# Norm boundaries at high priority, early decay scalars, masks behind q's reciprocal norm and late norm-row broadcasts in a two-block f32 kernel

## The chip, the cores and the metric

The kernel runs on one core of a Trainium2 chip. The metric is the device time of one execution in microseconds (us): the median of several executions, 932.28 us before the change (three runs, 931.84 to 934.05).

## What is computed

Input x is 256 rows of 1024 floats (f32), and two different blocks follow one another. Weights and activations are f32.

```
first block:
  h    = rms_norm(x, pre_mix_norm);  proj = h @ w_in            # q, k, v | gdn q, k, v | z | a, b
  mix  = concat(softmax_attention(q, k, v, rel_bias),           # causal, 8 heads of 64
                gated_deltanet(conv(gdn qkv), z, a, b)) @ w_out  # chunks of 64
  x    = x + rms_norm(mix, post_mix_norm)
  h    = rms_norm(x, pre_mlp_norm)
  x    = x + rms_norm(square(relu(h @ w_up)) @ w_down, post_mlp_norm)
second block:
  h    = rms_norm(x, g_mix);  proj = h @ w_in_2
  x    = x + (gate_a * conv(...) @ w_a_out + gate_r * retention(q, k, v, dec_f, dec_b) @ w_r_out) @ w_o
  h    = rms_norm(x, g_ffn)
  x    = x + (silu(h @ w_ff_gate) * (h @ w_ff_up)) @ w_ff_down
  return rms_norm(x, g_final)
```

In gated_deltanet each chunk of 64 rows needs the solution of a unit lower triangular system, (I + m) uw = rhs, where m comes from the normalized k; q is divided by its norm as well. In the retention every head has a decay, log_sigmoid(dec_f) and log_sigmoid(dec_b), of which the kernel forms log(1 + exp(-|.|)).

## The kernel before, in words

**Matrix products.** Every large product is taken in three matmuls with fp32r operands: high part by high part, high by low, low by high. `load_w` (L207 to L218) fetches a 512 KB weight tile `raw` by a DMA from SP's queue (three buffers), ACT copies its high part into `wh` (the copy is recorded at L144), and DVE subtracts it, `wl` = raw - wh (L218). PE works on wh and wl at L222, or L294 for one kind of product. The activations stand transposed in `xT`, again as a high part, which ACT writes (L413), and a low part, which DVE writes (L416). PE fills PSUM banks of three names: `mm`, `sd` and `at`.

**What sets the order.** A tile scheduler orders each engine's instructions by priority, which is program order unless the code says otherwise, and by what is ready. `after(name)` (L167 to L176) puts the next instructions of an engine behind the instruction last recorded under that name: an edge in the order, not a wait by itself. SP issues the weight DMAs; POOL issues the small loads and the broadcasts, and does some elementwise work and all powers (reciprocal square roots).

**The head (up to about 30 us).** The first normalized rows are transposed, the first weight tiles come in, and POOL issues small loads: `rows` (conv weights), `hs` (A_log, dt_bias), three 256 KB tiles of constants `cs`, `relT`, and the four broadcasts `wb` of 256 KB: `row_bcast` (L178 to L185) reads a norm row of 1024 floats into two tiles of 128 x 512, the same on all partitions. `chan` holds the conv weights transposed; `lpl` is the logarithm that the gates g need, `R` is made of g and cs.

**The deltanet part (45 to 100 us).** POOL makes `kbe` and `kd` (L873 to L878), k scaled in two ways. `inv_norm` (L782) sums squares (`ssq`) and calls `rstd` (L400 to L403): DVE writes `ms`, POOL raises it to the power -1/2, `rnq` for q. DVE then scales q (`fq`, `fqd`, `qn`, `qd`), PE transposes the result (L795). The product m = `md` goes through memory into blocks of 16: `mb`. Four masked copies `b` of m (128 x 512 each, L893 to L896) are made on POOL for the levels 16 and 32. The solve inside the blocks (L932 to L937) is a chain of 15 steps of two DVE operations, `tmpb` and `tb`; its result goes through memory to `U` and `T`, which PE multiplies with the masks b. The convolution's `acc` steps run on DVE beside this.

**The boundaries.** Behind w_out (L1066 to L1074), w_down (L1118 to L1123) and w_o (L1278 to L1286) the product of each row tile t = 0, 1 is normalized and added to x (`post_norm_add`, L452 to L460, with squares `junk`, the power `r` on POOL L428, `pw` and the new x; behind w_o a plain addition), then `rms_T` normalizes x into the rows `xs` (L439, L441) and `row_T` (L447 to L452) transposes them on PE (L451) and splits them into xT. T0 and T1 below are these transposes for t = 0 and t = 1. The next product begins behind T0.

**The decay scalars.** `head_scalars` (L485 to L492) loads dec_f_2 and dec_b_2, a few values on each partition, and `log1p_exp_neg_abs` (L497 to L508) takes `lpa` = |.|, `lpu` = exp, and `lpl`, a logarithm for which ACT loads another function table. Both stand in the program behind the up stage.

## Time and profile before

| | before |
|---|---|
| median of 3 runs | 932.28 us (931.84 to 934.05) |
| profiled execution, its time | 932.19 us |
| its span | 930.4 us |
| instructions | 13880 |
| mean granted clock of PE | 0.994 |
| PE busy | 902.0 us (97%) |
| weight loads of PE (PEld) | 770.2 us (83%) |
| DVE busy | 600.1 us (64%) |
| ACT busy | 475.2 us (51%) |
| POOL busy | 81.2 us (9%) |

The span runs from the first to the last instruction of the profiled execution; the execution's own time is 1.8 us longer. Busy shares say how long an engine worked, not whether something waited for it: PEld overlaps PE, and what an engine waits for stands in a view of its own. PEclk is the clock that was granted to PE as a share of 2.4 GHz; 0.50 is 1.2 GHz. In the rows of a timeline stand start, duration, engine, line, operation, output and inputs, shapes and the number of instructions that were put together; in square brackets the idle time of the engine ahead of it and what ended that. All times are us from the start of the span, unless marked otherwise.

### The profile page before, as it was taken

To read this page: it belongs to the slowest core of one execution; us is meant where nothing else is said; L and a number is where in the kernel's file an instruction comes from. 1 tells how busy PE (TensorE), PEld (TensorE's weight loads), DVE (VectorE), ACT (ScalarE), POOL (GpSimd) and SP (SyncE) were. 2 spreads that over 40 slices of the span, in tenths; PEclk is the share of its full clock that TensorE was granted. 3 is DMA by queue.
4 is the path that set the end of the run, shared out by engine and by line. 5 is a ranking of instruction groups with operands and counts; after the bars stand their busy time and mean duration, and the time that the engine had idled before them with its cause. 6 is when DMAs were issued, how large, how long until landed. Compare 5 with 4: busy or idle time off the path is not lost.

```text
span 930.4 us, 13880 instructions
## 1 busy us (share of the span) xinstructions
PE 902.0 (97%) x5397; PEld 770.2 (83%) x5397; DVE 600.1 (64%) x885; ACT 475.2 (51%) x722; POOL 81.2 (9%) x96
## 2 busy tenths in 40 slices
PE   5999999989999999999999999999999999999997
PEld 4788887778888888799988888888888788888886
DVE  3888555376887563868666687844557657666543
ACT  4774373356766453645445555444344546555432
POOL 4072001030000000203200000000000000000000
PEclk9999999999999999999999999999999999999999
DMA  9673663147676665577646457666474567666551
GB/s 274 183 184 67 161 211 91 46 144 209 193 203 203 222 196 182 155 220 214 182 119 176 132 165 201 181 203 190 165 229 141 159 203 205 189 191 184 183 179 46
DMA packets 177138, 162.41 MB, mean 175 GB/s; under 512 B 18940, under 2 KB 144168, under 8 KB 177072
## 3 DMA queue, kind: packets, MB, share of 16 engines
q1 hardware_dynamic: 175200, 156.49, 57.3%
q0 software_dynamic: 1728, 4.78, 1.6%
q8 instruction: 42, 0.69, 0.3%
q10 hardware_dynamic: 144, 0.26, 0.1%
q14 instruction: 24, 0.20, 0.1%
HBM read 158.59 MB, written 2.92 MB: 174 GB/s over the span
## 4 chain that ended last, share of the span: by engine, by line
PE 85%; DMA 4%; POOL 3%; ACT 3%; DVE 3%; issue 2%; SPq 0%; POOLq 0%; ACTq 0%
PE mm L222 57%; PE at L222 18%; PE sd L222 6%; PE mm L294 2%; DMA raw<-in_w_in_dram 1%; POOL b L147 1%; ACT junk L424 1%; DVE wl L218 1%; PE sd L795 1%; POOL r L428 1%; DMA rows<-in_w_conv_dram 1%; DMA raw<-in_w_up_dram 1%; ACT wh L144 1%; DMA wb<-in_pre_mlp_norm_dram 1%; DMA x<-in_x_dram 0%
## 5 line engine op out<-in xcount | busy, mean ns | idle before, releaser
L218 DVE TENSOR_TENSOR wl<-raw,wh 128x1024 fp32r<-128x1024 f32 (+1 forms) x287 | 352.3, 1232 | 220.7 <-ACT wh L144 218.8
L144 ACT ACTIVATE wh<-raw 128x1024 fp32r<-128x1024 f32 (+1 forms) x287 | 301.8, 1056 | 293.5 <-PE at L222 69.5
L222 PE MATMUL mm<-xT,wh 128*128 128x256 f32 (+1 forms) x976 | 251.5, 334 | 1.4 <-ACT wh L144 1.4
L222 PEld LDWEIGHTS mm<-xT,wh 128*128 128x128 f32 x976 | 167.2, 193 | 21.0 <-ACT wh L144 1.6
L222 PE MATMUL mm<-wh,xT 128*128 128x512 f32 x528 | 168.6, 393 | 2.6 <-DVE xT L416 1.5
L222 PEld LDWEIGHTS mm<-wh,xT 128*128 128x128 f32 x528 | 98.7, 188 | 25.3 <-DVE xT L416 2.8
L222 PE MATMUL mm<-xT,wl 128*128 128x256 f32 x400 | 111.9, 280 | 0.0
L222 PE MATMUL mm<-wl,xT 128*128 128x512 f32 x264 | 103.5, 392 | 0.6 <-DVE wl L218 0.6
L222 PE MATMUL at<-xT,wh 128*128 128x512 f32 x272 | 97.4, 398 | 0.0
L294 PE MATMUL mm<-xT,wl 128*128 128x256 f32 x288 | 82.9, 288 | 1.2 <-DVE wl L218 1.2
L222 PE MATMUL at<-xT,wl 128*128 128x256 f32 x272 | 76.1, 280 | 0.0
L222 PEld LDWEIGHTS mm<-xT,wl 128*128 128x128 f32 x400 | 75.4, 189 | 0.0
L222 PE MATMUL mm<-wh,hidh 128*128 128x512 f32 x162 | 63.3, 391 | 0.0
L222 PE MATMUL mm<-wl,hidh 128*128 128x512 f32 x162 | 63.2, 390 | 0.0
L222 PE MATMUL mm<-wh,hidl 128*128 128x512 f32 x162 | 63.0, 389 | 0.0
L222 PEld LDWEIGHTS at<-xT,wh 128*128 128x128 f32 x272 | 51.1, 188 | 12.4
L222 PEld LDWEIGHTS mm<-wl,xT 128*128 128x128 f32 x264 | 49.6, 188 | 11.4 <-DVE wl L218 1.5
L294 PEld LDWEIGHTS mm<-xT,wl 128*128 128x128 f32 x288 | 56.5, 196 | 1.6 <-DVE wl L218 1.6
L222 PEld LDWEIGHTS at<-xT,wl 128*128 128x128 f32 x272 | 51.3, 189 | 0.0
L428 POOL TENSOR_TENSOR r<-ms,neghalf 128x1 f32<-128x1 f32 x13 | 10.7, 823 | 436.2 <-DVE ms L150 436.2
L222 PEld LDWEIGHTS mm<-wh,hidl 128*128 128x128 f32 x162 | 30.4, 188 | 6.5
L222 PEld LDWEIGHTS mm<-wh,hidh 128*128 128x128 f32 x162 | 30.5, 188 | 5.8
(378 smaller groups left out, 1237.9 us busy)
## 6 DMA issues: line engine op xcount, KB each, us to landing
raw<-in_w_in_dram SPq DMA_DIRECT2D x116, 512.0 KB, 4.5
raw<-in_w_up_dram SPq DMA_DIRECT2D x32, 512.0 KB, 4.4
raw<-in_w_down_dram SPq DMA_DIRECT2D x32, 512.0 KB, 3.8
raw<-in_w_ff_gate_dram SPq DMA_DIRECT2D x22, 512.0 KB, 4.1
raw<-in_w_ff_up_dram SPq DMA_DIRECT2D x22, 512.0 KB, 3.9
raw<-in_w_ff_down_dram SPq DMA_DIRECT2D x22, 512.0 KB, 3.5
raw<-in_w_r_out_dram SPq DMA_DIRECT2D x16, 512.0 KB, 4.2
raw<-in_w_out_dram SPq DMA_DIRECT2D x8, 512.0 KB, 3.8
```

The source lines that it names most:

```text
L144: nc.scalar.activation(o, i, f, **kw)
L147: (eng or nc.vector).tensor_tensor(o, a, b, op=op)
L218: last["wl"] = nc.vector.tensor_tensor(L, raw, H.bitcast(F32), op=SUB)
L222: nc.tensor.matmul(o, a, b, start=start, stop=stop)
L294: last["step"] = nc.tensor.matmul(o, L[:, k, :], XH, start=False, stop=k == 7)
L424: last["sq"] = nc.scalar.activation(T2("junk", tag="j"), srcs[i], AF.Square, scale=1.0 / 32, accum_out=ss[:, i:i + 1])
L428: last["pow"] = nc.gpsimd.tensor_tensor(r, ms, neghalf[:, :1], op=ALU.pow)
L795: nc.tensor.transpose(ps[:, a * P:(a + 1) * P], src[:, a * P:(a + 1) * P], ident)
```

## The change

1. `row_bcast` gets an argument for the instruction behind which its DMAs are issued; the two broadcasts of boundary 1 (post_mix_norm, pre_mlp_norm: four DMAs, 1.05 MB) are issued behind the last kd.
2. `rstd` records its power, and the four masks b are placed behind it, that is behind q's.
3. `rms_T`, `post_norm_add` and the residual addition behind w_o run under the scheduler's high priority.
4. The decay scalars are loaded right behind A_log and dt_bias, ahead of the constants, and their logarithm starts behind the last relu recorded so far, that is behind the up stage.

```diff
--- before.py
+++ after.py
@@ -175,10 +175,10 @@
         else:
             yield
 
-    def row_bcast(name, eng=None):
+    def row_bcast(name, eng=None, gate="pow"):
         a = I[name]
         h = [xpool.tile([P, 512], F32, tag="wb", name=nm("wb"), bufs=4) for _ in range(2)]
-        with after("pow"):
+        with after(gate):
             for i in range(2):
                 (eng or nc.gpsimd).dma_start(h[i], bass.AP(tensor=a.tensor, offset=a.offset + i * 512,
                                                            ap=[[0, P], [1, 512]]))
@@ -400,7 +400,7 @@
     def rstd(o, ss, n, dim):
         ms = sm("ms", n)
         nc.vector.tensor_scalar(ms, ss, 1.0 / dim, EPS, op0=MUL, op1=ADD)
-        tt(o, ms, neghalf[:, :n], ALU.pow, nc.gpsimd)
+        last["rstd"] = nc.gpsimd.tensor_tensor(o, ms, neghalf[:, :n], op=ALU.pow)
 
     def split_T(ps, X, k0, t, scale=None):
 
@@ -442,7 +442,8 @@
         return xs
 
     def rms_T(xt, wb, X, t):
-        row_T(rms_row(xt, wb, t in FUSED), X, t)
+        with tc.high_priority():
+            row_T(rms_row(xt, wb, t in FUSED), X, t)
 
     def row_T(row, X, t):
         for i, xs in enumerate(row):
@@ -452,12 +453,13 @@
             split_T(ps, X, 4 * i, t)
 
     def post_norm_add(ps, wb, xt):
-        r = rms_of(ps)
-        tmp = [T2("pw", tag="n") for _ in range(2)]
-        for i in range(2):
-            tt(tmp[i], ps[i], wb[i], MUL)
-        for i in range(2):
-            stt(xt[:, GS[i]], tmp[i], r, xt[:, GS[i]], MUL, ADD)
+        with tc.high_priority():
+            r = rms_of(ps)
+            tmp = [T2("pw", tag="n") for _ in range(2)]
+            for i in range(2):
+                tt(tmp[i], ps[i], wb[i], MUL)
+            for i in range(2):
+                stt(xt[:, GS[i]], tmp[i], r, xt[:, GS[i]], MUL, ADD)
 
     xr = [rms_row(x[:, t, :], wb_pre, True, None) for t in range(2)]
     C0 = T2("cs")
@@ -492,12 +494,14 @@
         return h
 
     hs = head_scalars(("A_log", "dt_bias"))
+    dl = head_scalars(("dec_f_2", "dec_b_2"))
     load_consts(0, NMIX)
 
     def log1p_exp_neg_abs(src, n):
 
         a, u, w, l, d, rw = (sm("lp" + c, n) for c in "auwldr")
-        act(a, src, AF.Abs)
+        with after("relu"):
+            act(a, src, AF.Abs)
         act(u, a, AF.Exp, scale=-1.0)
         nc.vector.tensor_scalar(w, u, 1.0, None, op0=ADD)
         last["ln"] = nc.scalar.activation(l, w, AF.Ln)
@@ -873,7 +877,7 @@
     for t in range(2):
         kbe, kd = G2("kbe"), G2("kd")
         tt(h8(kbe), h8(kn[t]), hb(tile_h(FB, t)), MUL, nc.gpsimd)
-        tt(h8(kd), h8(kn[t]), hb(tile_h(ER, t)), MUL, nc.gpsimd)
+        last["kd"] = nc.gpsimd.tensor_tensor(h8(kd), h8(kn[t]), hb(tile_h(ER, t)), op=MUL)
         KBE.append(kbe)
         KD.append(kd)
 
@@ -892,7 +896,8 @@
         bl = []
         for s in (16, 32):
             b = G2("b")
-            tt(h8(b), h8(MM[t]), cb(f"lev{s}"), MUL, nc.gpsimd)
+            with after("rstd"):
+                tt(h8(b), h8(MM[t]), cb(f"lev{s}"), MUL, nc.gpsimd)
             bl.append(b)
         BL.append(bl)
 
@@ -1066,7 +1071,7 @@
     wout.rows(mix, 0, range(WT0, 8), True)
     wout.rows(mix, 1, range(wout.k, 8))
     ps = wout.ps
-    wb1, wb2 = row_bcast("post_mix_norm"), row_bcast("pre_mlp_norm")
+    wb1, wb2 = (row_bcast(n, gate="kd") for n in ("post_mix_norm", "pre_mlp_norm"))
     X = Both("xT")
     for t in range(2):
         post_norm_add(ps[t], wb1, x[:, t, :])
@@ -1093,7 +1098,7 @@
 
         def up_evac(i=i, hf=hf):
             r = G2("relu")
-            act(r, hf, AF.Relu)
+            last["relu"] = nc.scalar.activation(r, hf, AF.Relu)
             stt(hf, hf, 0.0, r, MAX, MUL)
             hv = hf.rearrange("p (j n) -> p j n", j=2)
             act(hid.h[i], hv, AF.Copy)
@@ -1102,7 +1107,6 @@
         gemm_wide(I["w_up"][0], 256 * i, X, hf, up_evac)
     load_consts(NMIX, 3)
 
-    dl = head_scalars(("dec_f_2", "dec_b_2"))
     lg = sm("lg", 8)
     lp = log1p_exp_neg_abs(dl, 8)
     stt(lg, dl, 0.0, lp, ALU.min, SUB)
@@ -1282,7 +1286,8 @@
     for t in range(2):
         for i in range(2):
             gs = slice(i * 512, (i + 1) * 512)
-            tt(x[:, t, gs], ps[t][i], x[:, t, gs], ADD)
+            with tc.high_priority():
+                tt(x[:, t, gs], ps[t][i], x[:, t, gs], ADD)
         rms_T(x[:, t, :], wb1, X, t)
     dump("x3", x[:, 0, :])
```

What the scheduler makes of it stands in the order of the instructions. The numbers in the names are those of buffers and differ between the two kernels.

On POOL, in the deltanet part: kbe and kd are the scaled k, wb the broadcast rows, rnq the powers for q, b the masks, m and cs their inputs. Before:

```order
L147 TENSOR_TENSOR kbe_749<-kn_549,fb_581 128x512
L147 TENSOR_TENSOR kd_750<-kn_549,er_579 128x512
L147 TENSOR_TENSOR b_816<-m_699,cs_171 128x512
L147 TENSOR_TENSOR b_818<-m_699,cs_171 128x512
L147 TENSOR_TENSOR b_820<-m_722,cs_171 128x512
L147 TENSOR_TENSOR b_822<-m_722,cs_171 128x512
L147 TENSOR_TENSOR rnq_798<-ms_799,neghalf 128x8
L147 TENSOR_TENSOR rnq_806<-ms_807,neghalf 128x8
```

and now:

```order
L147 TENSOR_TENSOR kbe_752<-kn_552,fb_584 128x512
L880 TENSOR_TENSOR kd_753<-kn_552,er_582 128x512
L183 DMA wb_2154<-in_post_mix_norm_dram 128x512
L183 DMA wb_2155<-in_post_mix_norm_dram 128x512
L183 DMA wb_2158<-in_pre_mlp_norm_dram 128x512
L183 DMA wb_2159<-in_pre_mlp_norm_dram 128x512
L403 TENSOR_TENSOR rnq_801<-ms_802,neghalf 128x8
L403 TENSOR_TENSOR rnq_809<-ms_810,neghalf 128x8
L147 TENSOR_TENSOR b_819<-m_702,cs_174 128x512
L147 TENSOR_TENSOR b_821<-m_702,cs_174 128x512
```

The broadcasts, which stood in the head around the first `tb`, come behind the last kd, and both rnq come ahead of the four masks, of which the first two are shown.

On PE at boundary 1, behind w_out: mm and at with wh, wl and mixg are the last matmuls of w_out for tile 1, sd and at with ident and xs are T0. Before:

```order
L222 MATMUL mm_1894<-wh_2099,mixgl_1717 128x512
L222 MATMUL at_1895<-wh_2099,mixgh_1715 128x512
L222 MATMUL at_1895<-wl_2100,mixgh_1715 128x512
L222 MATMUL at_1895<-wh_2099,mixgl_1717 128x512
L451 MATMUL sd_2193<-ident,xs_2178 128x128 x4
L451 MATMUL at_2202<-ident,xs_2179 128x128 x4
L222 MATMUL mm_2325<-wh_2291,xT_2159 128x512
L222 MATMUL mm_2325<-wl_2292,xT_2159 128x512
```

and now:

```order
L222 MATMUL mm_1897<-wh_2102,mixgh_1718 128x512
L222 MATMUL mm_1897<-wl_2103,mixgh_1718 128x512
L452 MATMUL sd_2196<-ident,xs_2181 128x128 x4
L452 MATMUL at_2205<-ident,xs_2182 128x128 x4
L222 MATMUL mm_1897<-wh_2102,mixgl_1720 128x512
L222 MATMUL at_1898<-wh_2102,mixgh_1718 128x512
L222 MATMUL at_1898<-wl_2103,mixgh_1718 128x512
L222 MATMUL at_1898<-wh_2102,mixgl_1720 128x512
```

T0 has moved ahead of the last four matmuls of w_out. At boundary 2 it moves ahead by six matmuls and at boundary 3 by 19. T1 comes behind 28 matmuls of the next product where it came behind 33; at boundaries 2 and 3 this number is 28 (27 before) and 18 (16 before).

On ACT at boundary 1, behind T0: junk are the squares of tile 1's new x, wh and relu belong to the up stage, xT is written from T1, and lpa to lpl are the decays' logarithm. Before:

```order
L144 ACTIVATE wh_2321<-raw_2319 128x1024
L424 ACTIVATE junk_2229,ss_2228<-x 128x512
L424 ACTIVATE junk_2231,ss_2228<-x 128x512
L144 ACTIVATE relu_2350<-mm_2325 128x512
L413 ACTIVATE xT_2159<-sd_2239 128x2x128
L413 ACTIVATE xT_2160<-sd_2239 128x2x128
L144 ACTIVATE lpa_3171<-hs_3167 128x8
L413 ACTIVATE xT_2161<-at_2248 128x2x128
L413 ACTIVATE xT_2162<-at_2248 128x2x128
L144 ACTIVATE lpu_3172<-lpa_3171 128x8
L503 ACT_TABLE_LOAD
L503 ACTIVATE lpl_3174<-lpw_3173 128x8
```

and now:

```order
L144 ACTIVATE wh_2318<-raw_2316 128x1024
L424 ACTIVATE junk_2232,ss_2231<-x 128x512
L424 ACTIVATE junk_2234,ss_2231<-x 128x512
L144 ACTIVATE wh_2324<-raw_2322 128x1024
L144 ACTIVATE relu_2353<-mm_2328 128x512
L413 ACTIVATE xT_2162<-sd_2242 128x2x128
L413 ACTIVATE xT_2163<-sd_2242 128x2x128
L413 ACTIVATE xT_2164<-at_2251 128x2x128
L413 ACTIVATE xT_2165<-at_2251 128x2x128
```

Both junk stand ahead of the third wh of the up stage (2321 before, 2324 now), and lpa to lpl are gone from here; they follow the last relu of the up stage.

## Rows read from the trace of the kernel before

**Rows 1.** Page: busy time of each engine, share of the span, instructions.

```profile
PE 902.0 (97%) x5397; PEld 770.2 (83%) x5397; DVE 600.1 (64%) x885; ACT 475.2 (51%) x722; POOL 81.2 (9%) x96
```

**Rows 2.** Waits of PE, whole run: us in total, times, longest us.

```profile
PE mm L222 <- DVE xT L416: 1.5, 3, 0.9
PE mm L222 <- ACT wh L144: 1.4, 1, 1.4
PE sd L222 <- DVE m L147: 1.3, 1, 1.3
PE sd L795 <- DVE qn L147: 1.2, 1, 1.2
...
PE mm L222 <- ACT xT L413: 1.1, 3, 0.5
PE sd L795 <- DVE hf L150: 0.7, 1, 0.7
...
PE sd L222 <- DMA U<-ud: 0.6, 1, 0.6
```

**Rows 3.** Windows: us, busy PE, PEld, DVE, ACT, POOL, PEclk, DMA share, GB/s.

```profile
12.00:22.70 10.70, 10.01 (x80) 8.78 (x78) 4.98 (x11) 3.21 (x8) 4.65 (x9) 1.00 1.07 339
25.90:29.20 3.30, 3.30 (x17) 3.30 (x16) 2.36 (x10) 3.27 (x5) 0.00 (x0) 0.50 0.65 177
...
72.00:74.00 2.00, 2.00 (x19) 2.00 (x18) 2.00 (x4) 0.00 (x0) 2.00 (x2) 1.00 0.74 86
```

**Rows 4.** DMA issues, 12 to 13 and 68 to 70 us: KB, us to landing.

```profile
raw<-in_w_in_dram SPq DMA_DIRECT2D x1, 512.0 KB, 10.4
...
mb<-md SPq DMA_DIRECT2D x1, 128.0 KB, 4.9
```

**Rows 5.** Timeline of DVE in the head: the next tile's low part.

```profile
28.87 1.22 DVE L218 TENSOR_TENSOR wl<-raw,wh 128x1024 fp32r<-128x1024 f32 x1
```

**Rows 6.** Timeline of POOL: broadcasts, masks, q's reciprocal norms.

```profile
15.45 1.10 POOL L183 DMA_DIRECT2D wb<-in_post_mix_norm_dram  x2 [0.90 <-DMA rows<-in_w_conv_dram]
...
64.98 8.00 POOL L147 TENSOR_TENSOR b<-m,cs 128x512 f32<-128x512 f32 x4
72.94 3.24 POOL L147 TENSOR_TENSOR rnq<-ms,neghalf 128x8 f32<-128x8 f32 x2
```

**Rows 7.** Timeline of DVE ahead of the solve.

```profile
69.51 2.32 DVE L218 TENSOR_TENSOR wl<-raw,wh 128x1024 fp32r<-128x1024 f32 x1
...
72.92 2.42 DVE L150 SCALAR_TENSOR_TENSOR acc<-mm,chan,acc 128x255 f32<-128x255 f32 x6
...
78.84 0.17 DVE L147 TENSOR_TENSOR tmpb<-mb,tb 128x15 f32<-128x15 f32 x1
```

**Rows 8.** Timelines of PE, DVE and ACT at boundary 1.

```profile
193.24 0.39 PE L222 MATMUL at<-wh,mixgl 128*128 128x512 f32 x1
193.47 0.60 PE L451 MATMUL sd<-ident,xs 128*128 128x128 f32 x4
...
194.74 0.50 PE L222 MATMUL mm<-wh,xT 128*128 128x512 f32 x1 [0.24 <-ACT xT L413]
...
196.36 0.73 PE L222 MATMUL mm<-wh,xT 128*128 128x512 f32 x2 [0.89 <-DVE xT L416]
...
205.12 0.63 PE L451 MATMUL sd<-ident,xs 128*128 128x128 f32 x4 [0.79 <-DVE xs L439]
...
192.69 0.88 DVE L441 TENSOR_SCALAR xs<-xs,r 128x512 f32<-128x512 f32 x2 [0.45 <-POOL r L428]
...
200.16 1.06 ACT L144 ACTIVATE wh<-raw 128x1024 fp32r<-128x1024 f32 x1 [1.82 <-DMA raw<-in_w_up_dram]
...
209.39 0.21 ACT L144 ACTIVATE lpa<-hs 128x8 f32<-128x8 f32 x1 [2.95 <-DMA hs<-in_dec_b_dram]
```

**Rows 9.** Timelines of DVE and PE at boundary 2: rows xs and T0.

```profile
376.85 0.87 DVE L441 TENSOR_SCALAR xs<-xs,r 128x512 f32<-128x512 f32 x2
...
378.39 0.60 PE L451 MATMUL sd<-ident,xs 128*128 128x128 f32 x4
```

## The prediction, made before the changed kernel was run

> **What bounds the kernel now.** I read the totals first, then PE's waits, then the stages around the changed code. The totals [rows 1] show PE busy for 902.0 us, 97% of the span of 930.4, and no other engine above 65% by itself (the weight loads, PEld, overlap PE). So the change can win only what PE does not do, some 28 us of idle time, and the stretches in which PE runs at half its clock. PE's waits [rows 2] name 7.8 of the 28 that the changed code can reach: 1.4 us for a wh (near 24 us), 1.3 for m (60 us), 1.2 for qn (77 us), 0.6 for U (98 us), and at the three boundaries, where a residual row is normalized and transposed, 1.5 us for the low half of xT, 1.1 for its high half, 0.7 for hf. Each is worth a tenth of a per cent or so. The profiled execution took 932.19 us, 0.1 below the median of 932.28; all sums are made against 932.2. A measurement can tell about 0.3% (2.8 us) from no change.
>
> **The broadcasts leave the head: 2.3 us.** From 12 to 22.7 us the transfers run at 339 GB/s with every DMA engine full [rows 3]. The weight tile issued at 12.3 us takes 10.4 us to land [rows 4], and PE, out of weights, waits for its wh. Four broadcasts of 256 KB go out in that stretch. Three are ahead of the tile's last bytes: 3 x 0.262 MB / 339 GB/s = 2.3 us by which the tile lands earlier. The next wl, now at 28.87 to 30.1 us [rows 5], stands on DVE behind a chain of small steps that begins after the tile's wl, so it comes 2.3 us earlier as well. PE finishes its older tile at the same time as now, so its wait for wh turns into a wait for that second wl, and PE is 2.3 us ahead behind it. The stretch at granted clock 0.50 (the lower of the two levels, 1.2 GHz) that follows the wait today (3.3 us, so up to 1.65 us lost, [rows 3]) may follow the new wait too; then 0.7 is left at 30 us, but the 1.3 us wait for m takes up nearly all of the difference, since m hangs on DVE. Bounds: nothing, if the tile is late for another reason; 2.3 + 1.65 = 3.95 if a half-clock stretch goes as well. I take 2.3. The two decay loads, a few KB, now stand before the cs loads on POOL's queue; an issue costs POOL 0.55 us [rows 6], so cs starts 1 to 2 us later. I cost this at nothing, because 1.05 MB that slowed cs is gone from the queue behind it; without that cover R, and the second wl behind it, would be 1 to 2 us later.
>
> **Reciprocal norms before masks: 1.2 us.** On POOL the four masks take 8.0 us, 2.0 each, from 64.98 on, and only then come the two rnq, 3.24 us, to 76.18 [rows 6]. DVE's last fq waits for the second. The masks also cost DVE: a wl beside them took 2.32 us [rows 7], against 1.22 alone [rows 5], so 1.1 each. With rnq first, the wl takes 1.22, the second ms is written by about 70.9, and two rnq of 1.6 end at 72.8. DVE then has six acc of the convolution to do, 2.42 us [rows 7], from 71.0 until 73.4, so fq comes at 73.4 and not at 76.2: 2.8 us earlier. The first step of the solve (tmpb), at 78.84 now [rows 7], would come at 76.0. PE's 1.2 us wait for qn goes; its next limit is U, which the solve makes and for which it waits 0.6 us today. Upper bound: both waits, 1.8. Lower bound: all four masks fall on two-input DVE work, 4 x 1.1 = 4.4 us of delay, less the 1.8 that the earlier rnq gives = -2.6. I take 1.2, the wait that is surely in the way. The four broadcast issues, now behind kd, take 4 x 0.55 = 2.2 us of POOL up to 67.2; rnq cannot start before the first ms, which stands just ahead of the wl at 69.51, so they cost nothing there. The Trainium skill ("SBUF — State Buffer", section "Who interferes with whom") says that a DVE instruction with two SBUF inputs contends with a GpSimd instruction that reads SBUF, while one with a single SBUF input does not. The 2.32 us wl agrees; by this rule masks beside the solve's steps would hold them up, and the sum would be rival B's 930.3 in place of 926.5.
>
> **Boundary 1 (after w_out): 1.8 us.** Tile 0's transposes stand four matmuls earlier on PE; a matmul here takes 0.23 us from start to start (193.24 to 193.47, [rows 8]). So PE reaches them at 193.47 - 0.92 = 192.55, but the rows xs are written at 193.13 and 193.57: a new stall of 0.58. In exchange the four matmuls cover the evacuation, and the waits for xT behind them go, 0.24 and 0.89 us. Gain 1.13 - 0.58, about 0.6. Tile 1: its squares stand today behind a wh that waits 1.82 us for its DMA, and PE waits 0.79 for the rows [rows 8]. Ahead of that wh they can start 2 us earlier, and the transposes come five matmuls (1.15 us) earlier: the 0.79 goes, 0.8. Last, the logarithm of the decays leaves this place: its first step, lpa, held ACT for 2.95 us on a late load of hs [rows 8] ahead of two evacuations and a table load. The 0.7 us wait for hf comes behind that; I take half, 0.4. Sum 1.8. Lower bound 0.3 (only part of the T1 wait goes), upper 2.7 (no stall, all of hf). The logarithm now runs on ACT behind the last relu of the up stage, where PE has weights queued and ACT, busy 51% of the run [rows 1], has room; its result is due only in the retention. I cost it at nothing; if it held PE up there as long as it holds ACT here, 2.95.
>
> **Boundaries 2 and 3: 0.4 us together.** Of the 2.6 us for both halves of xT [rows 2], 1.13 are boundary 1's; 1.47 are left. At boundary 2 the transposes move up by six matmuls, from 378.39 to 377.0, and the rows are written at 377.28 and 377.72 [rows 9]: a stall of 0.3. At boundary 3 they move up by 19, further than the rows can follow, so PE stalls again, some 0.5. Waits removed less stalls is 0.7; I take 0.4, since tile 1 gains nothing in either (its order against the matmuls moves by two at most). Bounds -0.6 and 1.5.
>
> **Sum.** 2.3 + 1.2 + 1.8 + 0.4 = 5.7 us: 932.2 - 5.7 = **926.5**. All terms at their upper bounds: 3.95 + 1.8 + 2.7 + 1.5, about 10, 922.2. All at their lower: 0 - 2.6 + 0.3 - 0.6, and the logarithm's 2.95, about -5.9, 938.1.
>
> **Rivals.**
> A. The head gains nothing: the tile is bound by its own packets, or what is gained goes to half-clock stretches that no later wait takes up. For it: PE will be short of weights there either way. Against it: 339 GB/s with full engines, in which the broadcasts are a third of the bytes. 926.5 + 2.3 = 928.8, on the edge between faster and same.
> B. The masks fall on the solve. Its 30 steps read two SBUF operands each. If the masks start at 72.8 and take 2.0 us each as now, they last until 81, 5 us into a solve that would start at 76. The term of 1.2 becomes -2.6: 926.5 + 3.8 = 930.3, no change. Against it: from 73.4 to 76 DVE does qn and qd, whose large operand is in PSUM; beside these a mask should take about half of 2.0 us, and then all are done by 77.
> C. Slower: the broadcasts, now issued at 65 to 67 us, are ahead of mb, the copy of the blocks that the solve starts from. mb is issued at 68.9 and lands 4.9 us later, at 73.8 [rows 4], 5 us before the solve. If its small pieces had to wait for all 1.05 MB, and these moved at the 86 GB/s that the stretch 72 to 74 us shows [rows 3], it would land 12.2 us later, at 86.0, 7.2 after the present start of the solve. PE would get U that much later and fall to half clock again (1.65); the other places give 2.3 + 2.2 back: 932.2 + 7.2 + 1.65 - 4.5 = 936.5. It decides the sign once the broadcasts move below about 98 GB/s. Against it: 339 GB/s in the head, at which they take 3.1 us. The Trainium skill ("DMA: Bandwidth & Descriptors", section "SWDGE vs HWDGE vs iDMA") says that each DMA engine goes round-robin between the queues that feed it; no row here shows the two queues at mb, and by that rule C would not happen.
> D. High priority moves instructions but wins nothing: the stalls for rows that come too late equal the waits removed at all boundaries. 926.5 + 2.2 = 928.7.
>
> **Chances.** Forecast 0.58, A 0.14 (half faster, half same), B 0.14 (same), C 0.08 (slower), D 0.06 (faster). Faster by over 0.3%: 0.58 + 0.07 + 0.06 = 0.71. Same: 0.07 + 0.14 = 0.21. Slower: 0.08. The range must hold A, B and D and most of the forecast's bounds: 922.5 to 931.5; C and the corners, in which several bounds meet, stay outside.
>
> **What would show it.** Head: the tile issued near 12.3 us lands in under 8.5 us, the wait for wh is gone, and one wait for wl of about 2 us stands near 26; wrong if the tile still takes 10. Masks: rnq end by 73, fq without a wait on POOL, tmpb by 77 and steps of about 0.2 us; wrong (B) if tmpb steps stretch beside b. mb: it lands before the first tmpb; wrong (C) if tmpb waits for it. Boundaries: the waits for xT gone, waits for xs of 0.3 to 0.6 us in their place, T1 of boundary 1 without a wait; wrong (D) if the xs waits sum to 2.5 us or more. The logarithm's rows stand near 290 us with PE full.

## The result and the profile after

The changed kernel took 927.98 us (median of 6 executions, 926.05 to 929.78) against 933.41 for the kernel before (median of 6, 931.84 to 934.48). The ratio is 0.9939, 95% interval 0.9921 to 0.9957: 0.6% faster. A later series gave 927.25 against 933.66, ratio 0.9929 (0.9911 to 0.9948). The forecast was 926.5 in a range of 922.5 to 931.5. One execution of a later kernel ("fq on POOL" below, 938.74 us) was in a slower state of the chip and counts in no number.

The page of the changed kernel, totals; they answer to [rows 1]. Its profiled execution took 928.00 us.

```profile
span 926.2 us, 13882 instructions
PE 899.7 (97%) x5397; PEld 768.6 (83%) x5397; DVE 600.2 (65%) x885; ACT 475.9 (51%) x722; POOL 78.8 (9%) x96
```

PE did the same 5397 matmuls. Of the 4.2 us by which the span is shorter, 2.3 are busy time (the same matmuls took less, with one stretch at half clock fewer) and 1.9 are waits. PE's waits over the whole run (us in total, times, longest) answer to [rows 2]:

```profile
PE sd L452 <- DVE xs L439: 10.4, 4, 9.4
PE mm L294 <- DVE wl L218: 1.8, 2, 1.0
PE sd L799 <- DVE qn L147: 1.6, 1, 1.6
PE sd L452 <- DVE xs L441: 1.2, 3, 0.5
PE mm L222 <- ACT wh L144: 1.2, 2, 0.6
PE sd L799 <- DVE tmpb L147: 0.9, 1, 0.9
...
PE sd L222 <- DVE m L147: 0.8, 1, 0.8
...
PE sd L222 <- DVE xT L416: 0.3, 1, 0.3
```

As forecast, the boundaries' waits for xT and the wait for hf are gone (the 0.3 left for xT is in the head, 0.4 before), and three waits of up to 0.5 us for xs stand in their place, in front of T0. U's wait is gone too, which the forecast had in its upper bound only; a second profile of the changed kernel has 0.9 there. Against the forecast, T1 still waits at all three boundaries (0.3, 0.2 and 0.5 us, in the first row with 9.4 of the head), the waits for wh and wl did not turn into one, qn's wait did not go but grew from 1.2 to 1.6, and a new one of 0.9 stands behind it: PE's second q transpose, put down to tmpb.

**Where the time went.** PE's matmuls can be counted in both traces, from 0, and the start of the n-th read off:

| matmul no. | place | before | after | after less before |
|---|---|---|---|---|
| 300 | behind the head | 55.84 | 55.62 | -0.2 |
| 1560 | ahead of boundary 1 | 187.35 | 186.25 | -1.1 |
| 1800 | behind boundary 1 | 238.55 | 234.85 | -3.7 |
| 2300 | ahead of boundary 2 | 336.90 | 333.20 | -3.7 |
| 2600 | behind boundary 2 | 404.69 | 400.65 | -4.0 |
| 4300 | ahead of boundary 3 | 719.19 | 715.13 | -4.1 |
| 4500 | behind boundary 3 | 763.19 | 759.07 | -4.1 |

In this pair of executions boundary 1 gives 2.6 of the 4.2 us, boundaries 2 and 3 give 0.4, and everything ahead of boundary 1 gives 1.1, where the forecast had 3.5. The head of the changed kernel, DVE and DMA. First the issue of the fourth weight tile (KB, us to landing), then its wl and the next:

```profile
raw<-in_w_in_dram SPq DMA_DIRECT2D x1, 512.0 KB, 9.7
```

```profile
23.09 1.23 DVE L218 TENSOR_TENSOR wl<-raw,wh 128x1024 fp32r<-128x1024 f32 x1 [5.79 <-ACT wh L144]
...
28.11 1.22 DVE L218 TENSOR_TENSOR wl<-raw,wh 128x1024 fp32r<-128x1024 f32 x1
```

The tile takes 9.7 us where it took 10.4 [rows 4], and the next wl comes 0.76 us earlier [rows 5], not 2.3. Granted clock by windows (columns as in [rows 3]):

```profile
29.90:33.10 3.20, 3.20 (x16) 3.20 (x16) 3.20 (x9) 1.26 (x2) 0.00 (x0) 0.50 0.58 166
63.20:66.60 3.40, 3.40 (x32) 3.40 (x31) 3.40 (x6) 2.93 (x5) 3.25 (x6) 1.00 0.90 201
```

One stretch at half clock is left ahead of the last microseconds, where the profile before had two, near 26 and near 63 us.

The solve's approach, POOL and DVE of the changed kernel:

```profile
67.84 4.18 POOL L403 TENSOR_TENSOR rnq<-ms,neghalf 128x8 f32<-128x8 f32 x2 [1.39 <-DVE ms L402]
72.00 4.97 POOL L147 TENSOR_TENSOR b<-m,cs 128x512 f32<-128x512 f32 x4
```

```profile
67.67 1.21 DVE L218 TENSOR_TENSOR wl<-raw,wh 128x1024 fp32r<-128x1024 f32 x1
...
72.06 1.25 DVE L908 TENSOR_SCALAR fq<-rnq 128x8 f32<-128x8 f32 x1 [0.68 <-POOL rnq L403]
73.23 1.30 DVE L147 TENSOR_TENSOR fqd<-fq,ec 128x8 f32<-128x8 f32 x1
74.46 0.68 DVE L147 TENSOR_TENSOR qn<-sd,fq 128x512 f32<-128x512 f32 x1
...
75.66 1.34 DVE L147 TENSOR_TENSOR fqd<-fq,ec 128x8 f32<-128x8 f32 x1
...
78.12 0.17 DVE L147 TENSOR_TENSOR tmpb<-mb,tb 128x15 f32<-128x15 f32 x1
```

rnq ends 4.2 us earlier than in [rows 6] and the wl is back to 1.21 us [rows 7]. But now fq and two fqd, operations of 0.15 us, take 1.25 to 1.34 beside the masks, and tmpb starts at 78.12 against 78.84: earlier by just the 0.7 us that the weight tiles ahead of it had gained.

Boundary 1, PE and ACT; the rows answer to [rows 8]:

```profile
192.14 0.66 PE L452 MATMUL sd<-ident,xs 128*128 128x128 f32 x4 [0.51 <-DVE xs L441]
...
199.06 0.50 PE L222 MATMUL mm<-wl,xT 128*128 128x512 f32 x1 [0.36 <-DVE wl L218]
...
201.56 0.63 PE L452 MATMUL sd<-ident,xs 128*128 128x128 f32 x4 [0.32 <-DVE xs L439]
```

```profile
289.57 0.20 ACT L144 ACTIVATE lpa<-hs 128x8 f32<-128x8 f32 x1
```

T0 waits 0.51 us for its rows (0.58 forecast), T1 0.32 (none forecast), and lpa runs at 289.57 with no wait.

### The profile page after: what moved, and what is told of

Same layout as the page of the kernel before. It is cut to its first block, busy times and chain, and to the rows that moved or that the text cites. A ratio compares the mean times of both kernels' runs of the same rounds, so it can differ in the third digit from the quotient of the medians.

```text
span 926.2 us, 13882 instructions
## 1 busy us (share of the span) xinstructions
PE 899.7 (97%) x5397; PEld 768.6 (83%) x5397; DVE 600.2 (65%) x885; ACT 475.9 (51%) x722; POOL 78.8 (9%) x96
## 4 chain that ended last, share of the span: by engine, by line
PE 85%; DVE 5%; DMA 3%; ACT 3%; issue 2%; POOL 1%; SPq 0%; POOLq 0%; DVEq 0%; ACTq 0%
PE mm L222 57%; PE at L222 18%; PE sd L222 6%; DMA raw<-in_w_in_dram 2%; PE mm L294 2%; DVE wl L218 2%; POOL r L428 1%; ACT wh L144 1%; ACT junk L424 1%; DVE acc L150 1%; PE sd L452 1%; PE sd L799 1%; DMA raw<-in_w_out_dram 1%; DMA x<-in_x_dram 0%; POOL rnq L403 0%
## 5 line engine op out<-in xcount | busy, mean ns | idle before, releaser
L294 PEld LDWEIGHTS mm<-xT,wl 128*128 128x128 f32 x288 | 55.9, 194 | 2.2 <-DVE wl L218 2.2
```

The costliest lines, as they stand in the source:

```text
L294: last["step"] = nc.tensor.matmul(o, L[:, k, :], XH, start=False, stop=k == 7)
```

## The experiments

Twelve kernels ran, in three series, each beside the kernel before. Two executions of one kernel differ by 1 to 10 us, so the table shows stages of the one profiled execution of each beside the ratio of all: when the fifth weight tile lands; the start of matmul 300; the start of the first tmpb less the start of the wl near 58 us (the fifteenth); boundary 1 as the time from matmul 1560 to matmul 1800; the mean granted clock of the timed executions; and the ratio to before with its interval.

| kernel | tile 5 lands | matmul 300 | tmpb less wl | boundary 1 | mean clock | ratio to before |
|---|---|---|---|---|---|---|
| before | 26.53 | 55.84 | 20.03 | 51.21 | 0.994 | 1 |
| changed | 23.70 | 55.62 | 20.04 | 48.60 | 0.997 | 0.9939 (0.9921 to 0.9957) |
| changed, again | 23.27 | 52.72 | 20.74 | 48.56 | 0.997 | 0.9929 (0.9911 to 0.9948) |
| u1, broadcasts back | 25.79 | 55.84 | 18.31 | 48.63 | 0.995 | 0.9955 (0.9936 to 0.9974) |
| u2, masks back | 23.20 | 53.95 | 20.02 | 48.55 | 0.995 | 0.9947 (0.9926 to 0.9968) |
| u3, no high priority | 24.73 | 55.30 | 20.06 | 49.15 | 0.995 | 0.9953 (0.9927 to 0.9980) |
| u4, decay scalars back | 23.52 | 54.76 | 20.99 | 53.99 | 0.995 | 1.0003 (0.9974 to 1.0032) |
| d, decay scalars alone | 24.85 | 55.04 | 20.05 | 49.33 | 0.994 | 0.9989 (0.9963 to 1.0014) |
| p, high priority alone | 26.85 | 56.28 | 20.03 | 53.98 | 0.992 | 1.0013 (0.9988 to 1.0038) |
| pd, both alone | 25.45 | 56.67 | 20.03 | 48.60 | 0.994 | 0.9970 (0.9955 to 0.9985) |
| zero fills late | 21.18 | 50.91 | 20.71 | 48.72 | 0.995 | 0.9919 (0.9886 to 0.9953) |
| fq on POOL | 22.87 | 51.80 | 19.33 | 48.51 | 0.997 | 0.9929 (0.9883 to 0.9976) |
| the same, broadcasts behind masks | 23.34 | 53.15 | 16.90 | 48.48 | 0.990 | 0.9999 (0.9977 to 1.0021) |
| the same, zero fills late too | 22.75 | 51.56 | 16.90 | 48.77 | 0.991 | 0.9966 (0.9943 to 0.9989) |

### Each part undone

**u1: the broadcasts back in the head.**

```diff
-    wb1, wb2 = (row_bcast(n, gate="kd") for n in ("post_mix_norm", "pre_mlp_norm"))
+    wb1, wb2 = row_bcast("post_mix_norm"), row_bcast("pre_mlp_norm")
```

> The changed kernel with the four broadcasts back in the head (its other parts kept). Theory Z: the tile issued at 12.3 us is late because it stands behind the two zero fills of 520 KB on SP's queue, and the broadcasts only slow all of them a little: its wl starts at 23.8 instead of 23.1, and the time is 0.8 us longer. Rival (the forecast): the broadcasts' bytes stand ahead of the tile: wl at 25.4, 2.3 us longer. Second rival: the 0.76 us came from elsewhere: wl stays at 23.1, no difference.

The issue of the fourth tile in this kernel (KB, us to landing):

```profile
raw<-in_w_in_dram SPq DMA_DIRECT2D x1, 512.0 KB, 8.0
```

All three theories missed: with the broadcasts back the fourth tile came faster than in the changed kernel, 8.0 us, and its wl started at 20.75. That tile says nothing of the broadcasts: in the five profiles that have them in the head it took 8.0 to 10.4 us, in the seven that don't (zero fills in place) 6.7 to 9.7. The bytes are paid by the next tiles. The fifth lands at 24.9 to 26.9 with the broadcasts (mean 25.9) and 22.9 to 24.7 without (23.5); the sixth at 27.9 to 28.8 (28.4) and 24.6 to 26.2 (25.5). That is 2.4 and 2.8 us, the forecast's 2.3 us on other tiles. PE feels it at matmul 300: mean 55.9 with (55.0 to 56.7), 53.9 without (51.8 to 55.6), so 2.0 us on average, and anything from -0.6 to 4.9 between two single executions.

This kernel also shows what the new place of the masks can give. Its tmpb comes 18.31 us behind the wl, 1.7 earlier than before, and PE's waits for qn are gone. DVE at the solve:

```profile
74.80 0.15 DVE L147 TENSOR_TENSOR fqd<-fq,ec 128x8 f32<-128x8 f32 x1
...
77.35 0.17 DVE L147 TENSOR_TENSOR tmpb<-mb,tb 128x15 f32<-128x15 f32 x1
77.55 1.15 DVE L942 TENSOR_TENSOR tb<-tb,tmpb 128x15 f32<-128x15 f32 x1
```

The second mask starts at 74.80 as well, and fqd is not held; in the changed kernel the two start at 73.25 and 73.23, and fqd takes 1.30. Here the masks hold the second fq (1.26) and one step of the solve, so that the solve ends 29.0 us behind the wl, against 30.0 before and 29.9 and 30.6 in the two profiles of the changed kernel. What decides who is held does not show.

**u2: the masks ahead of rnq again.**

```diff
     rq = [inv_norm(pq[t], "q") for t in range(2)]
+    last["rnq"] = last["rstd"]
...
-            with after("rstd"):
+            if True:
                 tt(h8(b), h8(MM[t]), cb(f"lev{s}"), MUL, nc.gpsimd)
...
-    wb1, wb2 = (row_bcast(n, gate="kd") for n in ("post_mix_norm", "pre_mlp_norm"))
+    wb1, wb2 = (row_bcast(n, gate="rnq") for n in ("post_mix_norm", "pre_mlp_norm"))
```

> The changed kernel with the four masks ahead of the two rnq again; the broadcasts, behind kd in the changed kernel, are put behind the second rnq so that nothing else changes for rnq. Theory M: what rnq gained, the masks take back from fq and fqd, which now run beside them (1.25, 1.30 and 1.34 us instead of 0.15): the first tmpb stays within 0.5 us of 78.1, PE waits once, 1.2 us, for qn and 0.6 for U, and the time is within 0.6 us of the changed kernel. Rival (the forecast): the order is worth 1.2 us or more, tmpb comes 1 to 3 us later and the time is longer by 1.2.

DVE of this kernel ahead of the solve:

```profile
67.25 2.32 DVE L218 TENSOR_TENSOR wl<-raw,wh 128x1024 fp32r<-128x1024 f32 x1
69.49 1.26 DVE L402 TENSOR_SCALAR ms<-ssq 128x8 f32<-128x8 f32 x1
...
74.03 0.16 DVE L147 TENSOR_TENSOR fqd<-fq,ec 128x8 f32<-128x8 f32 x1
...
76.58 0.17 DVE L147 TENSOR_TENSOR tmpb<-mb,tb 128x15 f32<-128x15 f32 x1
```

Theory M holds for the solve: tmpb comes 20.02 us behind the wl, against 20.04 in the changed kernel (20.74 in its second profile). The masks hold three DVE operations by 1.1 us each in both, two wl and an ms here, fq and two fqd there. But the ways to tmpb differ. With the masks first, as in the kernel before, it leads through POOL: four masks of 8.0 us in all, then both rnq, for which DVE stands idle in front of its second fq. That row in the kernel before:

```profile
76.21 0.17 DVE L903 TENSOR_SCALAR fq<-rnq 128x8 f32<-128x8 f32 x1 [0.79 <-POOL rnq L147]
```

In the changed kernel it leads through the three held operations on DVE. That both ways take 20.0 us is chance: u1, with the masks behind rnq as well, has 18.31. The ratio, 0.9947, does not tell this kernel from the changed one.

**u3: without high priority; u4: decay scalars where they were.** u3 takes out the three `with tc.high_priority():`. u4:

```diff
     hs = head_scalars(("A_log", "dt_bias"))
-    dl = head_scalars(("dec_f_2", "dec_b_2"))
...
-        with after("relu"):
-            act(a, src, AF.Abs)
+        act(a, src, AF.Abs)
...
+    dl = head_scalars(("dec_f_2", "dec_b_2"))
     lg = sm("lg", 8)
```

> The changed kernel without the three uses of high priority. Theory P: they make most of the 2.6 us won at boundary 1 and all of the 0.5 at boundaries 2 and 3: about 2.2 us longer, with the waits for xT back (0.2 and 0.9, 0.5 and 0.4, 0.4 and 0.2). Rival L: boundary 1's gain is the logarithm's departure from ACT: 0.5 us longer, and the start of the first w_down matmuls less than 0.3 us later ahead of boundary 2.

> The changed kernel with the loads of the decay scalars and their logarithm where they were. Theory P: ACT waits 2 to 3 us for the load in front of lpa, and PE gets its 0.75 us wait for hf back: 0.8 to 1.0 us longer. Rival L: 2 us or more longer. In the head nothing changes by over 0.3 us, since the two small loads ahead of cs were taken to cost nothing.

Rival L holds. Without high priority boundary 1 is only 0.55 us longer (49.15 against 48.60). With the decay scalars back it is 5.4 us longer, 2.8 longer than in the kernel before, and no gain is left that clears the interval (ratio 1.0003). Why is shown at p, below.

### One part alone

**d and p.** The kernel before with the fourth part alone, and with the third alone.

> The kernel before with the fourth part alone: decay scalars loaded in the head, their logarithm behind the last relu. Theory L (the load behind which lpa waits on ACT is what boundary 1 loses): from the last transposes of w_out's input at 186 us to the matmuls at 217 us the run is 2.0 to 2.2 us shorter than before, with the 0.75 us wait for hf and the 2.95 us stall of ACT gone and the waits for xT (0.24 and 0.89) still there; elsewhere as before. Total 2 us faster than before. Rival P (the forecast): 0.4 us faster.

> The kernel before with the third part alone, high priority. Theory L: tile 1's rows come earlier, but the load of the decay scalars is issued behind tile 1's power and takes 5 to 6 us to land as ever, so ACT stands longer in front of lpa (over 4 us), PE waits some 3.5 us for hf in place of 0.75, and boundary 1 is 2 to 3 us longer than before; boundaries 2 and 3 win 0.5 to 0.7 together. Total 1.5 to 2.5 us slower than before. Rival P (the forecast): boundary 1 wins 1.4 and the total is 1.8 faster.

PE's waits at boundary 1 in d (timeline of PE), and ACT behind T1:

```profile
195.57 0.50 PE L222 MATMUL mm<-wh,xT 128*128 128x512 f32 x1 [0.24 <-ACT xT L413]
...
197.20 0.73 PE L222 MATMUL mm<-wh,xT 128*128 128x512 f32 x2 [0.89 <-DVE xT L416]
...
205.15 0.63 PE L451 MATMUL sd<-ident,xs 128*128 128x128 f32 x4 [0.79 <-DVE xs L439]
```

```profile
205.82 0.66 ACT L413 ACTIVATE xT<-sd 128x256 fp32r<-128x256 f32 x2 [2.70 <-PE sd L451]
206.49 0.66 ACT L413 ACTIVATE xT<-at 128x256 fp32r<-128x256 f32 x2
```

All of PE's waits for rows and for xT are as before, and yet boundary 1 is 1.88 us shorter: ACT writes the second half of xT 3 us earlier and goes on to the next wh, and the wait of 0.75 us for hf is gone. Not all of the 1.88 is the logarithm's. 0.60 is a wait for a wl at 203.8 us that this profile lacks; it stands ahead of lpa, and no run tells whether the change removed it. From the start of T1 on, the stage is 1.1 us shorter. In p, ACT and PE at the same place:

```profile
212.04 0.21 ACT L144 ACTIVATE lpa<-hs 128x8 f32<-128x8 f32 x1 [4.42 <-DMA hs<-in_dec_b_dram]
```

```profile
214.24 0.66 PE L797 MATMUL sd<-ident,hf 128*128 128x128 f32 x4 [3.65 <-DVE hf L150]
```

Theory L's signs come, but not for its reason. ACT stands 4.42 us in front of lpa in place of 2.95, PE 3.65 us in front of hf in place of 0.75, and boundary 1 takes 53.98 us, 2.8 longer than before. The load did follow T1 forward: counted from matmul 1560, T1 starts 2.5 us earlier than before and the load is issued 2.5 us earlier too. The longer stand on ACT is the load's own time: dec_b took 6.0 us to land, against 4.5 before. What costs PE more is the order on DVE, here in the kernel before and then in p:

```profile
205.55 0.68 DVE L150 SCALAR_TENSOR_TENSOR hf<-mm,relu 128x512 f32<-128x512 f32 x1
...
210.17 0.76 DVE L416 TENSOR_TENSOR xT<-at,xT 128x256 fp32r<-128x256 f32 x2 [2.95 <-ACT xT L413]
```

```profile
212.83 0.76 DVE L416 TENSOR_TENSOR xT<-at,xT 128x256 fp32r<-128x256 f32 x2 [4.21 <-ACT xT L413]
213.50 0.68 DVE L150 SCALAR_TENSOR_TENSOR hf<-mm,relu 128x512 f32<-128x512 f32 x1
```

Priority has put T1's xT ahead of the first hf on DVE. xT waits for ACT, ACT for the load, and now hf waits with them. Behind its wait PE runs 3.4 us at half clock, up to 1.7 of the 2.8 us (an estimate: half of that stretch); u4 shows the same wait (3.62) and the same stretch. The total of p, 1.0013, does not clear its interval.

**pd: both.**

> The kernel before with the third and fourth part together (high priority, and decay scalars early), without the broadcasts' and the masks' move. Theory: the two make all that is sure: 2.6 us at boundary 1 and 0.5 at the others, 3.1 together, and the broadcasts and masks bring what is left of the changed kernel's gain, under 1.5 us. Rival (the forecast): the broadcasts and masks are worth 3.5 of it, and this kernel is 2.2 us faster than before.

Boundary 1 is 48.60 us, as in the changed kernel: these two parts make all of it. The ratio is 0.9970, 2.2 us of the median, which is what the rival (the forecast) said; the theory's 3.1 lies inside the interval as well. The changed kernel is 4.2 us faster in the same series (931.44 to 927.25). So the broadcasts and the masks are worth more than the theory gave them. In the two profiles 3.95 us of it stand at matmul 300 (56.67 and 52.72), with a stretch at half clock ahead of it in pd alone; the start of the solve shows no gain (20.03 us behind the wl in pd, 20.74 in the changed kernel). See the clock, below.

### What holds the head and the solve

**Zero fills late.** The fills of td and ud move from their place ahead of the fourth tile on SP's queue to behind the seventh.

```diff
-        nc.sync.dma_start(raw, w[k0 * P:(k0 + nk) * P, c0:c0 + ncol].rearrange("(k p) n -> p k n", p=P))
+        ld = nc.sync.dma_start(raw, w[k0 * P:(k0 + nk) * P, c0:c0 + ncol].rearrange("(k p) n -> p k n", p=P))
...
         n = len(started)
+        if n == 6:
+            last["raw6"] = ld
...
-    for d in (td, ud):
-        nc.sync.dma_start(d[:, :].rearrange("p (r n) -> p r n", r=5),
-                          zero[:, None, :208].to_broadcast([P, 5, 208]))
...
+    with after("raw6"):
+        for d in (td, ud):
+            nc.sync.dma_start(d[:, :].rearrange("p (r n) -> p r n", r=5),
+                              zero[:, None, :208].to_broadcast([P, 5, 208]))
```

> The changed kernel with the two zero fills of 520 KB, which stand ahead of the fourth weight tile on SP's queue, moved behind the seventh. Theory Z: the tile, which landed 3.7 to 5.7 us behind the second fill in every run so far whether the broadcasts were there or not, lands by 18 us instead of 22; PE's waits for its wh (0.6) and wl (0.8) go, the next ones (0.6 and 1.0) shrink since the chain behind chan starts earlier: 1.5 to 3 us faster than the changed kernel. Rival: the tile is limited by what all queues move, and lands at 20.5 or later: less than 0.8 us.

The fourth tile's issue in this kernel, and its wl:

```profile
raw<-in_w_in_dram SPq DMA_DIRECT2D x1, 512.0 KB, 5.5
```

```profile
18.95 1.23 DVE L220 TENSOR_TENSOR wl<-raw,wh 128x1024 fp32r<-128x1024 f32 x1 [1.67 <-ACT wh L144]
```

Theory Z holds for the tile: it lands in 5.5 us, and its wl starts 4.1 us earlier than in the first profile of the changed kernel and 0.8 earlier than in the second (19.79). PE waits for nothing between 14 and 44 us, and matmul 300 starts at 50.9. Whether the fills hold the tile by their place in the queue or by their bytes, no run separates. At the end 3.0 us are left against the first profile and 2.2 against the second, and in the ratio (0.9919) the interval covers the changed kernel.

**fq and fqd on POOL**, behind each rnq and ahead of the masks (`eighth` is a tile of 0.125; DVE's own fq and fqd go):

```diff
+    FQ = []
+    for t in range(2):
+        fq, fqd = sm("fq", 8), sm("fqd", 8)
+        tt(fq, rq[t], eighth, MUL, nc.gpsimd)
+        last["fqd"] = nc.gpsimd.tensor_tensor(fqd, fq, tile_h(EC, t), op=MUL)
+        FQ.append((fq, fqd))
...
-            with after("rstd"):
+            with after("fqd"):
```

> The changed kernel with fq and fqd computed on POOL between the two rnq and the masks, so that DVE does no small SBUF operation beside the masks. Theory M: the 3.4 us that fq and the two fqd lose beside the masks come back: the first tmpb starts 17 to 17.5 us behind the wl that starts at 58.1 in the changed kernel (20.05 us there and also with the masks ahead), PE's waits for qn (1.6) and for the second qn (0.9) shrink to under 0.8 together, 1.0 to 1.8 us faster. Rival: the masks only push on to the next DVE work, the first solve steps, and the gain is under 0.4.

DVE of this kernel:

```profile
71.37 0.68 DVE L147 TENSOR_TENSOR qd<-sd,fqd 128x512 f32<-128x512 f32 x1
74.38 1.23 DVE L147 TENSOR_TENSOR tmpb<-mb,tb 128x15 f32<-128x15 f32 x1 [2.33 <-DMA mb<-md]
```

Neither theory had this: DVE is done 3 us earlier, and then waits 2.33 us for mb. The tmpb behind it is held by a mask, as the rival said. With the broadcasts behind kd, mb lands 18.6 to 19.3 us behind the start of the wl; without them there, 14.2 to 15.2. The delay is not mb's own. It is in the write of m to memory that mb reads. That write's last two issues before, and in the changed kernel (KB, us to landing of the last):

```profile
md<-m SPq DMA_DIRECT2D x2, 128.0 KB, 2.5
```

```profile
md<-m SPq DMA_DIRECT2D x2, 128.0 KB, 7.1
```

In all six profiles with the broadcasts behind kd it takes 7.1 to 7.5 us and lands within 0.25 us of the last broadcast; in the other eight it takes 2.5 to 2.8. mb itself takes 4.5 to 5.2 in all. That is rival C's mechanism one transfer earlier, at about 4 us of its 12.2.

**The same with the broadcasts behind the masks**, and **with the zero fills late too** (`gate="bm"`, recorded at the masks).

> The kernel with fq and fqd on POOL and the four broadcasts issued behind the masks instead of behind kd. There DVE was done with qd at 72.05 and waited 2.33 us for mb, and ACT waited 3.73 us for a weight tile in front of qt. Theory C: both waits are the broadcasts' doing: mb lands 14 to 15.5 us behind the start of the wl at 58.1 (18.8 in the changed kernel, 19.3 in the kernel with fq on POOL), the first tmpb starts 16.8 to 17.5 us behind it (20.05 and 19.3), and the waits of PE for qt and U (1.4 and 1.7) go or halve: 1 to 2 us faster than with the broadcasts behind kd. Rival: mb's own copy is the limit: tmpb stays at 19 or later.

> The same with the zero fills behind the seventh weight tile too. Theory: the two gains stand behind one another on the path and add: head 2 to 4 us, solve 1 to 2, so 3 to 5 us faster than the changed kernel, about 0.989 of before. Rival: what the head gains is waited for again ahead of the solve or at U, and this is no faster than the better of the two alone.

DVE of the first of the two at the solve, and its stretches at half clock:

```profile
72.70 0.17 DVE L147 TENSOR_TENSOR tmpb<-mb,tb 128x15 f32<-128x15 f32 x1
72.91 1.15 DVE L948 TENSOR_TENSOR tb<-tb,tmpb 128x15 f32<-128x15 f32 x1
74.09 1.21 DVE L147 TENSOR_TENSOR tmpb<-mb,tb 128x28 f32<-128x28 f32 x1
75.33 1.20 DVE L948 TENSOR_TENSOR tb<-tb,tmpb 128x28 f32<-128x28 f32 x1
```

```profile
59.50:62.70 3.20, 3.20 (x15) 3.20 (x16) 3.20 (x8) 1.69 (x2) 2.50 (x3) 0.50 0.94 241
80.00:83.20 3.20, 3.20 (x16) 3.20 (x16) 2.22 (x10) 0.00 (x0) 0.00 (x0) 0.50 0.45 174
131.20:141.20 10.00, 10.00 (x87) 7.77 (x87) 3.44 (x10) 5.42 (x15) 0.00 (x0) 0.50 0.30 97
```

mb is in time and tmpb starts 16.90 us behind the wl, 3.1 earlier, as theory C said. It is no use: the masks hold three steps of the solve itself, 1.0 us each, which is rival B. PE still waits 1.5 us for U and 1.5 for at. And the kernel runs 16 us of its profile at half clock; it is no faster than before (0.9999). With the zero fills late too it is 0.9966. No version here beats the changed kernel clear of the interval.

### The clock

The executions of one kernel spread by 1 to 10 us, and the spread goes with the mean granted clock that each shows. Over the 198 timed executions that have a clock on record, each taken against the mean of its own kernel, 0.001 of mean clock goes with 0.84 us (correlation -0.79). The changed kernel has 0.997, before 0.994, and every kernel that lacks one of its parts 0.992 to 0.995. So by estimate 2 to 2.5 us of the gain of 5.4 to 6.4 is PE at half clock less often. Put to a common clock of 0.996 with that slope, the changed kernel is 4.5 us faster than before, u1 and u2 equal it to 0.3 us, u3 and pd are 1.0 to 1.1 slower, u4 5.2, and the two kernels with late zero fills 1.9 and 2.0 faster; each of these is uncertain by 1 us or more. Most stretches at half clock stand behind one of PE's larger waits: in the profile before behind 1.4 and 1.3 us [rows 2], in the changed one behind 0.6 and 1.0. But the wait of 1.6 us for qn in the changed kernel has none behind it. Why the broadcasts and the masks together spare about one of them stays open; no run changes a wait without moving others.

## Why the prediction was right, and where it was not

**The total** was right: 5.7 us forecast, 5.4 and 6.4 measured, well inside the range. In part that is luck. The 1.2 for the masks did not come; 0.8 more at boundary 1, and fewer stretches at half clock, which the forecast had in its upper bound only, made up for it.

**Broadcasts out of the head, 2.3.** The size was right on average, 2.0 us at matmul 300. The mechanism named the wrong tile: the fourth tile is held by two zero fills issued ahead of it on SP's queue, which the forecast did not see though they stand in the trace, and the broadcasts slow the fifth and sixth. The two profiles first compared showed 0.2 us at that matmul, within the spread of 4 us that the profiles without broadcasts in the head have.

**Reciprocal norms before masks, 1.2.** Wrong as a term of the path: in the changed kernel the start of the solve did not move (20.04 against 20.03; 20.74 in the second profile). The step that failed counted the masks against wl and against the solve's steps only, and took fq at 73.4 and tmpb at 76.0 as if fq and fqd cost nothing beside them: tiny as they are, they were held like the wl, 3 x 1.1 us, which took back what the earlier rnq gave. With the broadcasts in the head (u1) only one of the three was held, and 1.7 us came. So the term is not wrong by nature; it hangs on what DVE does beside each mask. The Trainium skill ("SBUF — State Buffer", section "Who interferes with whom") says that DVE and GpSimd share one pair of ports as an exclusive lock, that `tensor_tensor` with two SBUF inputs contends, and `tensor_scalar` when it enters a 2-port mode. The trace agrees for fqd (1.30 us), and fq, a tensor_scalar, took 1.25; qn, whose large input is in PSUM, kept its 0.68. In u1 the first fqd ran beside a mask in 0.15. The prediction told this rule without its exception for the 2-port modes. Rival B was this mechanism at another place, and its place came up in u1 (one step) and once fq was moved away (three). What u1's and u2's ratios lack against the changed kernel (about 1 to 2 us each) goes with their lower mean clock; the intervals overlap.

**Boundary 1, 1.8.** Measured 2.6, near the upper bound of 2.7, in every kernel with both parts. The waits that the forecast named gave the 1.8: 0.6 at T0 (0.24 and 0.89 less the new 0.51), 0.5 at T1 (0.79 to 0.32, where 0.8 was forecast), and all 0.75 of hf, of which the forecast took half. The other 0.8 was in no term: a wait for a wl is 0.24 shorter, and PE counts as busy for 0.5 us less. What failed is that the gains were summed as if they were independent: alone the logarithm's departure is worth 1.9 in its stage and priority loses 2.8, and on top of the other priority adds 0.7. The forecast did not ask what priority would put behind ACT's 2.95 us in front of lpa [rows 8].

**Boundaries 2 and 3, 0.4.** 0.4 in the first pair of profiles. From matmul 2300 to 2600, 67.8 to 67.9 us without priority and 67.3 to 67.7 with it, so 0.4 on average at boundary 2; at boundary 3 nothing that stands out of the spread (44.0 to 44.2 and 43.8 to 44.5).

**The logarithm's new place, 0.** Right: lpa runs at 289.57 without a wait.

**Rival C** came as a mechanism, but at a lower price and off the path: mb is 3.8 us later, near the 3.1 that 339 GB/s gave, and at 76.9 still 1.2 us ahead of tmpb. It was held through m's write, not through mb. The Trainium skill ("DMA: Bandwidth & Descriptors", section "SWDGE vs HWDGE vs iDMA") says that each DMA engine goes round-robin between its queues. In this trace m's write still landed with the last broadcast, so the prediction drew too much from that rule. **Rival D** was wrong: the waits for xs are 0.5, 0.2 and 0.5 us in front of T0, and with T1's 2.3 in all, under the 2.5 that would have borne it out, while the waits removed were larger.

## What to carry to other kernels

A small instruction that waits for a late load on an engine that works in order costs what is queued behind it, not its own time: look for what releases the load, and before moving work forward, look at what it will be put ahead of on each engine, since a stall that it carries along is then paid by more. An elementwise operation on POOL can hold one DVE operation that reads its data from SBUF for about a microsecond (the four masks held three before and in the changed kernel, two in u1), so a new place helps only where DVE has slack, or work that reads from PSUM. Where differences are a few tenths of a per cent, compare stage lengths between counted instructions over several profiles, and the mean granted clock beside the times.

## What the runs showed of the hardware that was not expected

- A DVE operation of 128x8 elements took 1.23 to 1.35 us beside a POOL multiply of 128x512, against 0.15 alone, and a wl of 128x1024 took 2.3 against 1.2: the same 1.1 us for both, near the 1.04 us that such a multiply (kd) takes.
- Two writes of 520 KB ahead of a 512 KB weight tile on one queue made the tile land in 6.7 to 10.4 us in twelve profiles; with the writes behind it, it took 5.5 and 5.9.
- A write of 128 KB on SP's queue, issued while POOL issued 1.05 MB of broadcasts, took 7.1 to 7.5 us to land, against 2.5 to 2.8, and landed with the last of them.
- One kernel's executions differ by up to 1%, and the longer ones show the lower mean granted clock: 0.001 goes with 0.84 us.
